# Paced table gathers, output tables on VectorE and scores in row halves, in a two-layer decoder trunk in float32

## The chip, the cores and the metric

One Trainium2 chip, one core. The metric is the time of one execution on the device, in microseconds (us). A trace is one execution taken by the hardware profiler; its span runs from the first to the last instruction, and the execution's own time is a little longer.

## The reference

256 tokens of width 1024 go through two layers. Each layer is: half a SwiGLU FFN (width 2816), a token mixer, half a second FFN, and a gated input embedding. Every sub-layer has a norm ahead of it and one behind. The mixer of layer 0 is differential attention with 8 heads of two maps each; that of layer 1 is a diagonal state-space model (S5) with 64 groups of 16 channels and 64 complex states, followed by GELU and a gated projection (GLU).

```python
# layer 0 mixer, per head, two maps m of 64 dimensions
s = einsum('bhmqd,bhmkd->bhmqk', q, k) + bias[t5_bucket(dist)]
prob = softmax(where(dist >= 0, s, -1e30))
attn = prob[:, :, 0] - lam * prob[:, :, 1]
o = rmsnorm(attn @ v, subln_g) * (1 - lambda_init)
m = o @ w_o
# layer 1 mixer, per group, complex diagonal recurrence
x[t] = a_bar * x[t-1] + b_bar @ u[t]
y[t] = (c @ x[t]).real + d * u[t]
z = gelu(y) @ w_glu + b_glu
m = z[:1024] * sigmoid(z[1024:])
```

## The kernel before

**Tiles and halves.** The tokens lie in two halves of 128 (b = 0 and 1). Each half is a generator (`thread(b)`), and a loop at the end of the program advances the two in steps, half 0 four to seven steps ahead (`lag`). One step of an FFN uses one weight unit of 512 KB: two slices of 128 rows, and for each three matmuls into 512 columns (`mm3`, L312 to L314).

**Weights.** Every float32 weight is loaded into a `raw` tile (SP's DMA queue, L124) and split into `hi` (ScalarE, L136) and `lo` = raw - hi (VectorE, L138). The three products hi x hi, lo x hi and hi x lo make up one float32 product. The class `Weights` takes loads up to 9 units (`NB`) ahead of half 1 (`W.next` is the next unit to load, `W.last_raw` the last load, `W.tiles` the split pairs); 9 split pairs and 3 raw tiles are kept.

**Order.** The program is ordered per engine ahead of the run by a list scheduler that simulates it, with priorities (`tc.high_priority`; a negative offset is a lower one). On the chip each engine then goes through its list in that order, and SP and GpSimd issue their DMAs from such lists. `tc.issue_after(i)` adds a dependence on instruction `i`.

**Norms.** `pre_norm` transposes x (L349), splits it (L331 on ScalarE, L332 on VectorE) and forms the factor on GpSimd (`v_pre`, `r_pre`, L325 and L327). `post_norm` squares on ScalarE (L380), forms `v_pn` and `r_pn` on GpSimd (L323, L327), and adds to x on VectorE (L387). The next `pre_norm` of that half begins with this x.

**Attention.** `attn_prepare` makes the table of biases in DRAM (`tab_d`) and two tiles `qz`, in which the two maps of a head's q stand in the upper and lower 64 rows with zeros in the other half. `scores(b, h)` does one head: a bias load on SP, two matmuls over all 128 rows (L596, two records each) into bank `a0` or `a1` by the parity of h, one addition, one maximum, two exponentials on ScalarE, and the combination of the maps on VectorE. `attend` (L619 to L625) uses the same banks.

**State-space tables.** `ssm_tables` is a generator. From the second FFN of layer 0 on, it is advanced at low priority at every second step of half 1 (`every`; a number yielded replaces it). For each of 8 group pairs `gp` it makes `vr`, `vi` by six products of 128x512 (L907 to L912, on GpSimd), transposes them (L933) and multiplies them in column quarters (L940) on TensorE, and stores `v_d`; then it makes `or`, `oi` by six further products on GpSimd in the same two tiles, and stores `o_d` from SP (L956). After that, eight DMAs write `m_d` (L972) and eight gathers of 512 KB build `t_d` from it (L975), all from GpSimd. `load_v` brings the first four `V` tiles in from SP (L1250), emitted when the loads come within 8 units of the mixer's first unit. The mixer of layer 1 reads `V`, `t_d` and `o_d`.

Of the kernel before, what the change touches and what calls it, by code (L numbers as in the profile page):

```python
# [9 lines left out]
F32 = mybir.dt.float32  # L10
# [3 lines left out]
ALU = mybir.AluOpType  # L14
# [54 lines left out]
TABLE_EVERY = OPT.get("every", 3)  # L69
PREPARE_AT = 36  # L70
# [77 lines left out]
def trunk(ctx, tc, x, p, norm_g, ffn_w_in, ffn_w_out, attn_w_qkv, attn_w_o, attn_lam, attn_subln_g,  # L148
# [377 lines left out]
    def attn_prepare():  # L526
        raw2_cm.__exit__(None, None, None)
        at_["pool"] = attn_pool_cm.__enter__()
        at_["qz"] = qz = [at_["pool"].tile([P, 4, 2, P], F32, tag=f"qz{b}", name=f"qz{b}", bufs=1) for b in range(2)]
        for b in range(2):  # L530
            nc.gpsimd.memset(qz[b][0:64, :, 1, :], 0.0)
            nc.gpsimd.memset(qz[b][64:128, :, 0, :], 0.0)
# [51 lines left out]
    def scores(b, h):  # L584
        kT = shared["kT"]
        nk = P * (b + 1)
        nm = f"{h}_{b}"
        bias = at_["pool"].tile([P, 2, 256], F32, tag="bias", name=f"bias{nm}", bufs=3)
        src = at_["tab_d"][2 * h:2 * h + 2, 256 - nk:256 - nk + 1]
        with tc.issue_after(W.last_raw.ins) if b == 0 and h < 3 else nullcontext():  # L590
            nc.sync.dma_start(bias[:, :, 0:nk], bass.AP(tensor=src.tensor, offset=src.offset,
                                                          ap=[[1, P], [384, 2], [1, nk]]))
        sp = bank(f"a{h % 2}", f"sp{nm}")
        spv = sp[:, :2 * nk].rearrange("p (m k) -> p m k", m=2)
        for m in range(2):
            nc.tensor.matmul(spv[:, m], at_["qz"][b][:, h % 4, m, :], kT[:, h, 0:nk], start=True, stop=True)  # L596
        s = at_["pool"].tile([P, 2, 256], F32, tag="s", name=f"s{nm}", bufs=3)
        sv = s[:, :, 0:nk]
        nc.vector.tensor_tensor(sv, spv, bias[:, :, 0:nk], ALU.add)
        mx = small.tile([P, 2], F32, tag="mx", name=f"mx{nm}")  # L600
        nc.vector.tensor_reduce(mx, sv, AX.X, ALU.max, negate=True)
        z = small.tile([P, 2], F32, tag="z", name=f"z{nm}")
        for m in range(2):
            nc.scalar.activation(s[:, m, 0:nk], s[:, m, 0:nk], AF.Exp, bias=mx[:, m:m + 1], accum_out=z[:, m:m + 1])
        rz = small.tile([P, 2], F32, tag="rz", name=f"rz{nm}")
        nc.vector.reciprocal(rz, z)
        c1 = small.tile([P, 1], F32, tag="c1", name=f"c1{nm}")
        nc.vector.tensor_tensor(c1, rz[:, 1:2], at_["neg_lam"], ALU.mult)
        at = weights_of(b, h)
        nc.vector.tensor_scalar(at, s[:, 0, 0:nk], rz[:, 0:1], None, ALU.mult)  # L610
        nc.vector.scalar_tensor_tensor(at, s[:, 1, 0:nk], c1, at, ALU.mult, ALU.add)
# [15 lines left out]
    def attention(b, qkv_units, pj_units, o_units):  # L627
# [33 lines left out]
        for n, (part, grp) in enumerate(QKV_ORDER):  # L661
# [21 lines left out]
            if part == 0:  # L683
                for m in range(2):
                    (nc.vector.tensor_copy if m >= OPT["qz"] else nc.scalar.copy)(
                        at_["qz"][b][64 * m:64 * m + 64, :, m, :], ptv[64 * m:64 * m + 64, :, ::-1])
            else:
                nc.vector.tensor_copy(kT[:, grp * 4:grp * 4 + 4, b * P:(b + 1) * P], ptv)
                for h in range(grp * 4, grp * 4 + 4):
                    with tc.high_priority(offset=HEAD_OFFSET):  # L690
                        scores(b, h)
# [74 lines left out]
    def ssm_tables(pool, keep):  # L766
# [137 lines left out]
        def products(out_r, out_i, ar_, ai_, br_, bi_, nm):  # L904
            g = nc.gpsimd
            t = pool.tile([P, 512], F32, tag="pt", name=f"pt{nm}", bufs=1).rearrange("p (q k h) -> p q k h", q=4, k=8)
# [11 lines left out]
        for gp in range(8):  # L918
# [4 lines left out]
            products(vr, vi, *A, *B, f"v{gp}")  # L923
# [24 lines left out]
            yield  # L948
# [395 lines left out]
```

## Time and profile before

| | |
|---|---|
| time, median of 3 runs (lowest to highest) | 1120.79 us (1118.37 to 1122.93) |
| profiled execution: time, span | 1120.96 us, 1119.2 us |
| busy: TensorE (PE), weight load (PEld) | 1043.0 us, 835.7 us |
| busy: VectorE (DVE), ScalarE (ACT), GpSimd (POOL) | 696.5 us, 553.8 us, 255.4 us |
| mean granted clock of TensorE | 0.975 of full |
| moved by DMA | 218.62 MB |

Busy times are sums over instructions of one engine. Matmuls overlap each other in the record, so the spacing of their starts tells more than their durations. Half 0 starts the gated embedding of layer 0 (`gt`, tiles `gtple`) at about 547 us, and the products of half 0 of the next FFN begin at about 590 us.

### The profile page before, as it was taken

What the parts mean: (1) busy time and instruction counts of PE and PEld (TensorE: products, weight loads), DVE (VectorE), ACT (ScalarE), POOL (GpSimd) and SP (SyncE); (2) the same over time, 40 slices, a digit from 0 to 9 for tenths busy, and PEclk for the clock granted to TensorE, in tenths of its full rate; (3) what the DMA queues carried; (4) which work ended last, traced back from release to release, by engine and by line L of the source; (5) the groups of instructions that cost most, each with busy time, mean ns of one, the idle gap of its engine ahead of it and who ended that gap; (6) DMA issues with size and microseconds to landing.
All of it is one profiled execution on the core that took longest, in us unless ns stands there. A gap on an engine that the chain in (4) does not pass through costs nothing. (4 is left out here: it accounts for less than half of the span.)

```text
span 1119.2 us, 14344 instructions
## 1 busy us (share of the span) xinstructions
PE 1043.0 (93%) x5123; PEld 835.7 (75%) x5123; DVE 696.5 (62%) x1011; ACT 553.8 (49%) x875; POOL 255.4 (23%) x315
## 2 busy tenths in 40 slices
PE   7999999999989999999778998999768899999996
PEld 5888888787766887777556886888546778888885
DVE  6656645688568986554686663654377676555464
ACT  6545444566655544443464543543335465444454
POOL 1002100100011018887788530000131010000001
PEclk9999999999999999999898999999989999999999
DMA  9656656476366777666564778766874647665651
GB/s 328 197 149 189 210 189 201 144 235 201 106 144 185 207 179 233 208 194 216 157 181 118 211 236 307 247 198 206 225 308 166 204 148 215 188 186 180 198 168 57
DMA packets 119816, 218.62 MB, mean 195 GB/s; under 512 B 25025, under 2 KB 43489, under 8 KB 119745
## 3 DMA queue, kind: packets, MB, share of 16 engines
q1 hardware_dynamic: 116864, 211.71, 60.9%
q0 software_dynamic: 1824, 5.33, 1.7%
q8 instruction: 40, 0.66, 0.2%
q10 hardware_dynamic: 1056, 0.66, 0.2%
q14 instruction: 32, 0.25, 0.1%
HBM read 205.13 MB, written 16.74 MB: 198 GB/s over the span
## 5 line engine op out<-in xcount | busy, mean ns | idle before, releaser
L138 DVE TENSOR_TENSOR lo<-raw,hi 128x1024 fp32r<-128x1024 f32 x332 | 429.6, 1301 | 266.3 <-ACT hi L136 264.7
L136 ACT CAST hi<-raw 128x1024 fp32r<-128x1024 f32 x332 | 347.3, 1052 | 327.1 <-PE up L314 106.5
L312 PE MATMUL up<-hi,xThi 128*128 128x512 f32 x704 | 279.3, 400 | 5.2 <-ACT hi L136 2.9
L313 PE MATMUL up<-lo,xThi 128*128 128x512 f32 x704 | 278.8, 397 | 1.5 <-DVE lo L138 1.4
L314 PE MATMUL up<-hi,xTlo 128*128 128x512 f32 x704 | 279.0, 400 | 0.0
L312 PEld LDWEIGHTS up<-hi,xThi 128*128 128x128 f32 x704 | 133.9, 190 | 34.8 <-ACT xThi L331 4.3
L313 PEld LDWEIGHTS up<-lo,xThi 128*128 128x128 f32 x704 | 134.1, 190 | 31.1 <-DVE lo L138 3.6
L314 PEld LDWEIGHTS up<-hi,xTlo 128*128 128x128 f32 x704 | 133.5, 191 | 28.1 <-issue 0.4
L312 PE MATMUL dn<-hi,hThi 128*128 128x512 f32 x352 | 139.2, 396 | 0.0
L313 PE MATMUL dn<-lo,hThi 128*128 128x512 f32 x352 | 138.5, 393 | 0.0
L314 PE MATMUL dn<-hi,hTlo 128*128 128x512 f32 x352 | 138.4, 394 | 0.0
L312 PEld LDWEIGHTS dn<-hi,hThi 128*128 128x128 f32 x352 | 66.8, 190 | 14.2 <-issue 0.6
L314 PEld LDWEIGHTS dn<-hi,hTlo 128*128 128x128 f32 x352 | 66.7, 190 | 14.3 <-issue 0.2
L313 PEld LDWEIGHTS dn<-lo,hThi 128*128 128x128 f32 x352 | 66.8, 190 | 13.6
L331 ACT ACTIVATE xThi<-xT_ps,gT 128x128 fp32r<-128x128 f32 x112 | 38.2, 368 | 59.2 <-PE xT_ps L349 58.3
L323 POOL TENSOR_SCALAR v_pn<-sspn,sspn 128x1 f32<-128x1 f32 x8 | 3.4, 422 | 246.8 <-ACT junkpn L380 244.7
L335 ACT CAST hThi<-hT_ps 128x512 fp32r<-128x512 f32 (+1 forms) x48 | 26.4, 550 | 56.2 <-PE hT_ps L459 56.0
L336 DVE TENSOR_TENSOR hTlo<-hT_ps,hThi 128x512 fp32r<-128x512 f32 (+1 forms) x48 | 30.8, 643 | 36.8 <-ACT hThi L335 36.7
L332 DVE SCALAR_TENSOR_TENSOR xTlo<-xT_ps,gT,xThi 128x128 fp32r<-128x128 f32 x112 | 36.1, 344 | 26.0 <-ACT xThi L331 25.5
L349 PE MATMUL xT_ps<-ident,x 128*128 128x128 f32 x112 | 30.3, 305 | 22.4 <-DVE xTlo L332 9.9
L349 PEld LDWEIGHTS xT_ps<-ident,x 128*128 128x128 f32 x112 | 16.2, 150 | 32.6 <-DVE xTlo L332 13.4
L456 DVE SCALAR_TENSOR_TENSOR h<-up,r_pre,sg 128x512 f32<-128x512 f32 (+1 forms) x48 | 33.6, 702 | 10.7 <-ACT sg L454 7.3
(360 smaller groups left out, 1319.5 us busy)
## 6 DMA issues: line engine op xcount, KB each, us to landing
raw<-in_ffn_w_in_dram SPq DMA_DIRECT2D x160, 512.0 KB, 4.4
raw<-in_ffn_w_out_dram SPq DMA_DIRECT2D x88, 512.0 KB, 3.9
raw<-in_attn_w_qkv_dram SPq DMA_DIRECT2D x24, 512.0 KB, 4.4
raw<-in_ffn_w_in_dram SPq DMA_DIRECT2D x32, 256.0 KB, 3.7
raw<-in_ple_w_gate_dram SPq DMA_DIRECT2D x16, 512.0 KB, 3.5
raw<-in_ssm_w_glu_dram SPq DMA_DIRECT2D x16, 512.0 KB, 4.1
gain<-in_norm_g_dram SPq DMA_DIRECT2D x8, 512.0 KB, 4.8
raw<-in_attn_w_o_dram SPq DMA_DIRECT2D x8, 512.0 KB, 4.2
```

The costliest lines, as they stand in the source:

```text
L136: nc.scalar.copy(hi, raw)
L138: (nc.gpsimd if n in self.on_pool else nc.vector).tensor_tensor(lo, raw, hi.bitcast(F32), ALU.subtract)
L312: nc.tensor.matmul(out_ap, st_hi, w_hi, start=start, stop=False)
L313: nc.tensor.matmul(out_ap, st_hi, w_lo, start=False, stop=False)
L314: nc.tensor.matmul(out_ap, st_lo, w_hi, start=False, stop=stop)
L323: nc.gpsimd.tensor_scalar(v, parts[0], parts[1], eps, ALU.add, ALU.add)
L331: return (nc.scalar.activation(hi, psum, AF.Copy, scale=scale).ins, nc.vector.scalar_tensor_tensor(lo, psum, scale, hi.bitcast(F32), ALU.m ...
L332: nc.vector.scalar_tensor_tensor(lo, psum, scale, hi.bitcast(F32), ALU.mult, ALU.subtract).ins)
L335: nc.scalar.copy(hi, psum)
L336: nc.vector.tensor_tensor(lo, psum, hi.bitcast(F32), ALU.subtract)
L349: marks[b].append(nc.tensor.transpose(pt, xb[:, k * P:(k + 1) * P], ident).ins)
L456: nc.vector.scalar_tensor_tensor(h[:, :w], up_, r, sg[:, :w], ALU.mult, ALU.mult)
```

## The change

It does four things.

Attention: `scores` takes two heads at a time. The `qz` tiles and their zeros go; q stands unpadded in one tile, written by one copy. Each map is a matmul over its own 64 rows, map 0 into bank `a0` and map 1 into bank `a1`, both heads side by side in a bank. The bias load, the maximum, the reciprocal and the factor are done once for two heads.

Tables: the six products for `or`, `oi` go from GpSimd to VectorE, with tiles of their own (`or`, `oi`, `po`). The generator is advanced every third step of half 1 during the group pairs.

Gathers: the `m_d` writes wait until the loads have come 24 units into the first FFN of layer 1. Each `t_d` gather is bound to a one-element copy on GpSimd that reads the newest split tile, and one is emitted every four steps.

V loads: from 16 units ahead of the mixer's first unit on, one load per step, each bound to the last weight load. The scratch for GpSimd's DMA descriptors is set to 8192 bytes.

```diff
+V_AHEAD = 16
+TD_FROM = 24
@@ attn_prepare
-        at_["qz"] = qz = [at_["pool"].tile([P, 4, 2, P], F32, tag=f"qz{b}", name=f"qz{b}", bufs=1) for b in range(2)]
-        for b in range(2):
-            nc.gpsimd.memset(qz[b][0:64, :, 1, :], 0.0)
-            nc.gpsimd.memset(qz[b][64:128, :, 0, :], 0.0)
+        at_["q"] = [at_["pool"].tile([P, 4, P], F32, tag=f"q{b}", name=f"q{b}", bufs=1) for b in range(2)]
@@ scores
-    def scores(b, h):
+    def scores(b, h0):
+        kT, q = shared["kT"], at_["q"][b]
...
+        bias = at_["pool"].tile([P, 2, 2, 256], F32, tag="bias", name=f"bias{nm}", bufs=2)
+        src = at_["tab_d"][2 * h0:2 * h0 + 4, 256 - nk:256 - nk + 1]
+        with tc.issue_after(W.last_raw.ins) if b == 0 and h0 < 4 else nullcontext():
+            nc.sync.dma_start(bias.rearrange("p h m k -> p (h m) k")[:, :, 0:nk], bass.AP(
+                tensor=src.tensor, offset=src.offset, ap=[[1, P], [384, 4], [1, nk]]))
-        sp = bank(f"a{h % 2}", f"sp{nm}")
-        spv = sp[:, :2 * nk].rearrange("p (m k) -> p m k", m=2)
-        for m in range(2):
-            nc.tensor.matmul(spv[:, m], at_["qz"][b][:, h % 4, m, :], kT[:, h, 0:nk], start=True, stop=True)
+        sp = [bank(f"a{m}", f"sp{nm}{m}")[:, :2 * nk].rearrange("p (h k) -> p h k", h=2) for m in range(2)]
+        for h in range(2):
+            for m in range(2):
+                rows = slice(64 * m, 64 * m + 64)
+                nc.tensor.matmul(sp[m][:, h], q[rows, (h0 + h) % 4, :], kT[rows, h0 + h, 0:nk], start=True, stop=True,
+                                 skip_group_check=True)
+        s = at_["pool"].tile([P, 2, 2, 256], F32, tag="s", name=f"s{nm}", bufs=2)
         for m in range(2):
+            nc.vector.tensor_tensor(s[:, :, m, 0:nk], sp[m], bias[:, :, m, 0:nk], ALU.add)
+        mx = small.tile([P, 4], F32, tag="mx", name=f"mx{nm}")
+        nc.vector.tensor_reduce(mx, s.rearrange("p h m k -> p (h m) k")[:, :, 0:nk], AX.X, ALU.max, negate=True)
...
@@ attention
-                for m in range(2):
-                    (nc.vector.tensor_copy if m >= OPT["qz"] else nc.scalar.copy)(
-                        at_["qz"][b][64 * m:64 * m + 64, :, m, :], ptv[64 * m:64 * m + 64, :, ::-1])
+                nc.vector.tensor_copy(at_["q"][b], ptv[:, :, ::-1])
...
-                for h in range(grp * 4, grp * 4 + 4):
+                for h in range(grp * 4, grp * 4 + 4, 2):
                     with tc.high_priority(offset=HEAD_OFFSET):
                         scores(b, h)
@@ ssm_tables
-        def products(out_r, out_i, ar_, ai_, br_, bi_, nm):
-            g = nc.gpsimd
-            t = pool.tile([P, 512], F32, tag="pt", name=f"pt{nm}", bufs=1).rearrange("p (q k h) -> p q k h", q=4, k=8)
+        def products(g, tag, out_r, out_i, ar_, ai_, br_, bi_, nm):
+            t = pool.tile([P, 512], F32, tag=tag, name=f"pt{nm}", bufs=1).rearrange("p (q k h) -> p q k h", q=4, k=8)
...
-            products(vr, vi, *A, *B, f"v{gp}")
+            products(nc.gpsimd, "pt", vr, vi, *A, *B, f"v{gp}")
...
-            yield
-            o_r = pool.tile(shp, F32, tag="vr", name=f"or{gp}", bufs=1)
-            o_i = pool.tile(shp, F32, tag="vi", name=f"oi{gp}", bufs=1)
+            yield 3
+            o_r = pool.tile(shp, F32, tag="or", name=f"or{gp}", bufs=1)
+            o_i = pool.tile(shp, F32, tag="oi", name=f"oi{gp}", bufs=1)
...
-            products(o_r, o_i, *A, *C, f"o{gp}")
+            products(v, "po", o_r, o_i, *A, *C, f"o{gp}")
...
-            yield
+            yield 3
...
-        yield 1
+        while W.next < flat(plan[("ffn", 1, 0)])[0] + TD_FROM:
+            yield 1
         for k in range(8):
             nc.gpsimd.dma_start(m_d[:, :, 7 + k, :], m16[16 * k:16 * k + 16])
         yield 2
+        pace = pool.tile([1, 8], F32, tag="zt", name="pace", bufs=1)
         for s_ in range(8):
-            nc.gpsimd.dma_start(t_d[16 * s_:16 * s_ + 16].rearrange("i g (c x) -> i (g c) x", x=P),
+            n = max(W.tiles)
+            gate = nc.gpsimd.tensor_copy(pace[:, s_:s_ + 1], W.tiles[n][0].bitcast(F32)[0:1, 0:1])
+            with tc.issue_after(gate.ins):
+              nc.gpsimd.dma_start(t_d[16 * s_:16 * s_ + 16].rearrange("i g (c x) -> i (g c) x", x=P),
                               m_d.rearrange("i g k o -> i g (k o)")[:, :, 16 * s_:16 * s_ + P])
-            yield 2
+            yield 4
@@ load_v and the loop over the steps
-                nc.sync.dma_start(ssm["V", pr][j], v_d[2 * pr + j])
+                with tc.issue_after(W.last_raw.ins):
+                    nc.sync.dma_start(ssm["V", pr][j], v_d[2 * pr + j])
+                yield
...
-        if has_ssm and "pool" in ssm and ("V", 0) not in ssm and W.next >= plan[("ssm",)][0][0] - OPT["vl"]:
-            load_v()
+        if has_ssm and "pool" in ssm and b == 1 and W.next >= plan[("ssm",)][0][0] - V_AHEAD:
+            ssm.setdefault("loads", load_v())
+            next(ssm["loads"], None)
...
-    nc = _bacc.Bacc("TRN2", target_bir_lowering=False, num_devices=1)
+    nc = _bacc.Bacc("TRN2", target_bir_lowering=False, num_devices=1, dynamic_dma_scratch_size=8192)
```

## Rows read from the trace of the kernel before

**Rows 1.** Page, busy us (share) and instructions; then span and granted clock.

```profile
PE 1043.0 (93%) x5123; PEld 835.7 (75%) x5123; DVE 696.5 (62%) x1011; ACT 553.8 (49%) x875; POOL 255.4 (23%) x315
...
core 0: 1119.2 us, clock 0.975
```

**Rows 2.** Windows of three stretches; columns as in the first line.

```profile
core 0: us, PE busy (x) PEld busy (x) DVE busy (x) ACT busy (x) POOL busy (x), PEclk, DMA share, GB/s
413.00:545.00 132.00, 121.76 (x612) 95.50 (x611) 74.55 (x58) 56.80 (x78) 108.76 (x85) 0.98 0.68 206
520.00:620.00 100.00, 81.82 (x383) 60.18 (x382) 65.37 (x71) 50.47 (x95) 78.93 (x70) 0.88 0.51 149
680.00:700.00 20.00, 16.94 (x67) 13.21 (x68) 9.48 (x10) 8.90 (x10) 0.00 (x0) 0.91 0.80 272
```

**Rows 3.** TensorE groups, 520 to 620 us, last 440 to 520: busy, mean, idle.

```profile
L349 PE MATMUL xT_ps<-ident,x 128*128 128x128 f32 x30 | 9.0, 316 | 12.4 <-DVE xTlo L332 8.6 <-DVE x L387 3.8
...
L933 PE MATMUL v_ps<-ident,vi 128*128 128x128 f32 x16 | 4.4, 298 | 5.5 <-POOL vi L912 5.5
...
L933 PE MATMUL v_ps<-ident,vi 128*128 128x128 f32 x12 | 3.1, 286 | 4.1 <-POOL vi L912 4.1
```

**Rows 4.** Timeline of GpSimd: start us, us, operation.

```profile
413.74 1.28 POOL L910 TENSOR_TENSOR vi<-ai,br 128x512 f32<-128x512 f32 x1
...
539.40 1.27 POOL L323 TENSOR_SCALAR v_pn<-sspn,sspn 128x1 f32<-128x1 f32 x1
540.65 1.25 POOL L912 TENSOR_TENSOR oi<-oi,pto 128x512 f32<-128x512 f32 x1
541.87 0.57 POOL L327 TENSOR_TENSOR r_pn<-v_pn,neg_half 128x1 f32<-128x1 f32 x1
...
624.94 1.66 POOL L912 TENSOR_TENSOR oi<-oi,pto 128x512 f32<-128x512 f32 x1
```

**Rows 5.** By line, ns min/median/max: 440 to 640 us, L1128 whole span.

```profile
L910 POOL TENSOR_TENSOR oi<-ai,cre x7: 1099/1111/2090, 460.1 to 619.0; 128x512 f32<-128x512 f32 x7
...
L138 DVE TENSOR_TENSOR lo<-raw,hi x51: 1207/1655/2353, 439.6 to 635.7; 128x1024 fp32r<-128x1024 f32 x51
...
L1128 DVE TENSOR_TENSOR rthi<-rtlo,er x2: 679/679/679, 823.3 to 839.8; 128x512 f32<-128x512 f32 x2
...
L1128 DVE TENSOR_TENSOR rt<-rt,er x2: 1034/1040/1046, 830.3 to 846.1; 128x512 f32<-128x512 f32 x2
...
L383 DVE TENSOR_TENSOR ygpnple<-mple,gain x4: 1522/1586/1779, 571.5 to 599.2; 128x512 f32<-128x512 f32 x4
```

**Rows 6.** Timeline of GpSimd: the gathers, and its next work for others.

```profile
665.44 6.01 POOL L975 DMA_DIRECT2D t_d<-m_d  x8 [3.46 <-DMA m_d<-msb]
...
787.79 0.35 POOL L990 MEMSET ssm_sel<- 128x128 f32 x2 [115.83 <-PE dn L314]
```

**Rows 7.** Groups, TensorE, 680 to 700 us.

```profile
L312 PE MATMUL up<-hi,xThi 128*128 128x512 f32 x22 | 9.1, 434 | 2.9 <-ACT hi L136 2.9
...
L313 PE MATMUL up<-lo,xThi 128*128 128x512 f32 x20 | 8.6, 428 | 0.8 <-DVE lo L138 0.8
```

**Rows 8.** Timeline of TensorE around the products of two heads, half 1.

```profile
244.08 0.39 PE L313 MATMUL qkvat<-lo,xThi 128*128 128x512 f32 x1
244.31 1.89 PE L596 MATMUL sp<-attn_hi,qz 128*128 128x256 f32 x8
...
246.49 0.39 PE L313 MATMUL qkvat<-lo,xThi 128*128 128x512 f32 x1
```

**Rows 9.** Timeline of TensorE around four products in column quarters.

```profile
518.82 0.39 PE L314 MATMUL dn<-hi,hTlo 128*128 128x512 f32 x1
...
520.18 0.40 PE L314 MATMUL dn<-hi,hTlo 128*128 128x512 f32 x1
...
520.62 0.43 PE L940 MATMUL m_ps<-vr,cp 128*32 128x128 f32 x8
...
521.56 0.40 PE L314 MATMUL dn<-hi,hTlo 128*128 128x512 f32 x1
```

More of the change, by code (lines that the diff above doesn't have):

```diff
@@ L582, in weights_of @@
         return shared["at"][h] if b else shared["at"][8 + h // 2][:, (h % 2) * P:(h % 2) * P + P]
-    def scores(b, h):
-        kT = shared["kT"]
+    def scores(b, h0):
+        kT, q = shared["kT"], at_["q"][b]
         nk = P * (b + 1)
[L587 to L592, printed above, removed]
-        sp = bank(f"a{h % 2}", f"sp{nm}")
-        spv = sp[:, :2 * nk].rearrange("p (m k) -> p m k", m=2)
-        for m in range(2):
-            nc.tensor.matmul(spv[:, m], at_["qz"][b][:, h % 4, m, :], kT[:, h, 0:nk], start=True, stop=True)
[L597 to L602, printed above, removed]
-        for m in range(2):
-            nc.scalar.activation(s[:, m, 0:nk], s[:, m, 0:nk], AF.Exp, bias=mx[:, m:m + 1], accum_out=z[:, m:m + 1])
-        rz = small.tile([P, 2], F32, tag="rz", name=f"rz{nm}")
-        nc.vector.reciprocal(rz, z)
[L607 to L611, printed above, removed]
@@ new lines, in scores @@
+        nm = f"{h0}_{b}"
+        bias = at_["pool"].tile([P, 2, 2, 256], F32, tag="bias", name=f"bias{nm}", bufs=2)
[4 more added lines that the diff above has]
+        sp = [bank(f"a{m}", f"sp{nm}{m}")[:, :2 * nk].rearrange("p (h k) -> p h k", h=2) for m in range(2)]
@@ new lines, in scores @@
+        nc.vector.tensor_reduce(mx, s.rearrange("p h m k -> p (h m) k")[:, :, 0:nk], AX.X, ALU.max, negate=True)
+        z = small.tile([P, 4], F32, tag="z", name=f"z{nm}")
+        for j in range(4):
+            part = s[:, j // 2, j % 2, 0:nk]
+            nc.scalar.activation(part, part, AF.Exp, bias=mx[:, j:j + 1], accum_out=z[:, j:j + 1])
+        rz = small.tile([P, 4], F32, tag="rz", name=f"rz{nm}")
+        nc.vector.reciprocal(rz, z)
+        c1 = small.tile([P, 2], F32, tag="c1", name=f"c1{nm}")
@@ L613, in attend @@
+        nc.vector.tensor_scalar(c1, rz.rearrange("p (h m) -> p h m", m=2)[:, :, 1], at_["neg_lam"], None, ALU.mult)
+        for h in range(2):
+            at = weights_of(b, h0 + h)
+            nc.vector.tensor_scalar(at, s[:, h, 0, 0:nk], rz[:, 2 * h:2 * h + 1], None, ALU.mult)
+            nc.vector.scalar_tensor_tensor(at, s[:, h, 1, 0:nk], c1[:, h:h + 1], at, ALU.mult, ALU.add)
     def attend(b, h, on):
@@ L1306, in trunk @@
             tables_step()
-        if has_ssm and "pool" in ssm and ("V", 0) not in ssm and W.next >= plan[("ssm",)][0][0] - OPT["vl"]:
-            load_v()
+        if has_ssm and "pool" in ssm and b == 1 and W.next >= plan[("ssm",)][0][0] - V_AHEAD:
+            ssm.setdefault("loads", load_v())
+            next(ssm["loads"], None)
         if state == ["join", "join"]:
             end_tables()
-            if ("V", 0) not in ssm:
-                load_v()
+            for _ in ssm.setdefault("loads", load_v()):
+                pass
             pool = ssm["pool"]
```

## The prediction

> **What bounds the kernel now.** I read the busy times first, then the windows along the span, then for each window in which TensorE is not full the groups that were idle before they ran, and last the order of time on the engine that was waited for. TensorE works 1043.0 of 1119.2 us at a mean granted clock of 0.975 [rows 1], so a change can win in two ways only: by closing its 76 us of gaps, or by keeping its clock at the upper of the two levels (2.4 GHz). The reader should see where those gaps lie. From 520 to 620 us it works 81.8 of 100 us at a clock of 0.88, and from 680 to 700 us 16.9 of 20 at 0.91 [rows 2]. In the first of these the idle time is 12.4 us ahead of the transposes of x at L349 and 5.5 us ahead of the transposes of `vi` at L933, and there are another 4.1 us of the latter kind from 440 to 520 [rows 3].
>
> What is late there is GpSimd. It makes the state-space tables: per group six products for `v` and six for `o`, 96 in all, from 413.7 to 626.6 us [rows 4]. TensorE meets each `v` inside the stream of weights, in an order fixed ahead of the run, and stands until the product lands. The norms suffer too: `v_pn` and `r_pn`, which release x, stand between two products (539.4, then a product at 540.7, then 541.9) [rows 4]. Each product is slower than it need be: one form takes between 1.10 and 2.09 us, and VectorE's split `lo` between 1.21 and 2.35 us in the same stretch [rows 5]. Both are drawn out by about one instruction of the other engine, so the two engines take turns.
>
> In the second place the eight gathers of `t_d` leave GpSimd within 6.0 us [rows 6], weights come late, and TensorE waits 2.9 and 0.8 us for a split [rows 7].
>
> **The change, part by part.**
>
> *Output tables on VectorE.* 48 of the 96 products leave GpSimd, and `or`/`oi` get tiles of their own, so `v` of the next group need not wait until `o` has gone out. A group now comes every six steps of half 1 in place of four. A step is one weight unit for both token halves: 2 slices x 3 products x 2 halves = 12 products. From 518.82 to 520.18 us seven of them start 0.227 us apart [rows 9], so a step is 2.72 us, six are 16.3 us, and eight groups 131 us. Begun at 414 us they end near 545 us, about where the chain behind the waits of L349 begins; before, they ran to 627 us, through the whole of that chain.
>
> Waits for `v`: 4.1 + 5.5 = 9.6 us. Between two meetings GpSimd ran twelve products and now runs six, so half the overrun (4.8 us) would stay; the longer period takes some more. I keep 3 and win 6.6.
>
> Waits of the norms: 12.4 us, in four places. I keep 1 us for each and win 8.4.
>
> Clock: 100 us at 0.88 mean 12.0 us not granted [rows 2]. It fell behind the longer of those waits. I keep 3 and win 9.
>
> Together 24.0; bounds: half of the 34.0 us there, 17, if the tables still reach into the norms, and all 34.0.
>
> *What VectorE pays.* The trace has no such product on VectorE. The nearest rows are products of 128x512 out of SBUF: 0.68 us free, 1.04 beside some GpSimd work, 1.59 in the thick of it [rows 5]. 48 of them cost 33, 50 or 76 us. From 413 to 545 us VectorE is busy 74.6 of 132 us [rows 2], so 57.4 are free. I take 1.04, since GpSimd will run half its products: 50 us fit, at 94%. I charge 2.5 us for splits that come late behind such a product, between 0 and the 19 us by which 76 overshoots. Behind a late product on SP stand the `o_d` stores, and behind these weight loads; raw and split buffers cover that, and without them it is the same late split.
>
> *Paced gathers.* Each gather waits on GpSimd for a one-element copy of the newest split. They start when the loads are 24 units into the next FFN (half 1 nine units behind, unit 15), then one every four steps, 10.9 us, for 76 us in place of 6. Behind the waiting copy on GpSimd stand only further gathers and set-up: its next work for anyone else was at 787.8 us [rows 6]. The four V loads, held behind a weight load each, follow at about half 1's step 46 of the 66 of that FFN. Removed: 2.9 + 0.8 us and 20 x 0.09 = 1.8 us of clock [rows 2, 7], 5.5 in all; a lone gather of 0.5 MB beside a weight load may still cost something, so I win 5.0 (between 4 and 5.5). If V came late instead, the first state products wait; 20 steps, 54 us, stand between. The halved DMA scratch is taken at nothing: if descriptors wait for room, only GpSimd's idle stretch pays.
>
> *Scores in row halves.* Before, the products of two heads of half 1 stand among weight products that would have taken 3 x 0.227 = 0.68 us alone and take 246.49 - 244.08 = 2.41 [rows 8]: 1.73 us, 0.86 a head. Half 0 has half as many columns, so 0.43. Eight heads of each make 10.3 us. If the two row halves run side by side this halves, a gain of 5.2; if in turn, nothing. The trace shows no row halves, only column quarters: one transpose and four such products stretch three products' 0.68 us to 1.38, by 0.70 [rows 9]. Four products of 128 columns one after another would cost 0.86 (two heads of half 0), so the quarters do overlap; a perfect overlap is 0.22, and at most 0.48 goes for getting in and out. Eight pairs x 0.48 = 3.8. Net 1.4, between 5.2 and -3.8.
>
> The Trainium skill, TensorEngine Tiling (Array Packing), section Key Properties, says against this part that a change of tiling mode drains the array. The trace agrees as far as the 0.48 us goes. By a full drain at each pair and no overlap this term would be -3.8 in place of 1.4.
>
> A pair now fills both banks `a0` and `a1`, so the next pair waits for both additions where heads alternated. QKV products of the other half hide that; uncovered it is two additions of about 0.68 [rows 5] per pair, 11 us in all, which I take at nothing. The single copy for q, the shared reductions and reciprocals, the absent memsets and the half as many bias loads on SP only relieve VectorE, GpSimd and SP; no gap listed above ends on them, so they too count nothing.
>
> **Sum.** The profiled execution took 1120.96 us, its span 1119.2 and 1.8 around it, 0.2 from the median of 1120.79. 1120.96 - 24.0 - 5.0 - 1.4 + 2.5 = 1093.1, say 1093.
>
> **Rivals.**
>
> *The shared door stays full.* Taking turns, not GpSimd's count, may be what sets the pace. From 413.7 to 626.6 us a group took 26.6 us. At free prices it cost 12 x 1.10 for products and, at the 51 splits in 200 us of [rows 5], 6.8 splits at 1.21: 21.4 of 26.6 us. Afterwards 6 x 1.10 + 6 x 0.68 and 4.2 splits (at that rate) to 6 (one a step) at 1.21 make 15.8 to 17.9 of 16.3 us: fuller than before. For it speaks how much both engines are drawn out [rows 5]; against it, that VectorE falls behind without TensorE standing as long as split buffers last. Then half of the 24.0 is won: 1120.96 - 12 - 5 - 1.4 + 2.5 = 1105.
>
> The Trainium skill, SBUF — State Buffer, section SBUF: two separate sides, states this as a rule: the port pair that VectorE and GpSimd share is an exclusive lock, held for the whole instruction, when the VectorE instruction has two SBUF inputs. The trace agrees (2.09 against 1.10 us), and by it the time would be that 1105.
>
> *The tables are not what is late.* The norms of this stage have few matmuls beside them, and their chains over ScalarE and VectorE could be long without GpSimd. Then only the gathers and the scores pay: 1120.96 - 5 - 1.4 + 2.5 = 1117. Against it, GpSimd stands directly in the chain at 539 to 542 us [rows 4].
>
> *VectorE becomes the bound: slower.* It decides where 48 products exceed the 57.4 us free, at 1.20 us each. At the 1.59 us row they overrun by 19 us; splits come late by that much, the loop again runs into the norms so that nothing of the 24.0 is won, and the clock falls as it does now, 12.0 us for 17.9 us of waits, another 12.7. 1120.96 + 19 + 12.7 - 5 - 1.4 = 1146. Against it, with GpSimd half empty the thick case should be the rarer.
>
> **Chances.** Forecast 0.63, full door 0.17, only the gathers 0.11, VectorE the bound 0.09. A difference of 0.5%, 5.6 us, is about what a measurement of this kernel can tell from none. The first two are faster (0.80), the third within 0.5% (0.11), the fourth slower (0.09). The forecast's own range is 1076 (34.0 + 5.5 + 5.2 won, nothing paid) to 1108 (17 + 4 won, 3.8 + 4 paid). The range reaches to the third case, 1076 to 1117, and leaves out the slow one and a little at either end.
>
> **What would show it.** Right: GpSimd's busy time down by 70 us or more from 255; the last table product near 545 us, not 627; `lo` in that stretch nearer 1.4 than 1.66 us; waits of L933 below 4 us and of L349 in the next norms below 5; clock above 0.95 there and 0.98 overall; the gathers spread over 70 us and no wait for a split at 680; a pair of half 1 costing about 1.2 us of TensorE. Wrong: table products on VectorE of 1.5 us, waits of TensorE for `lo` or `hTlo` from 413 to 545 us, tables that still run at 600 us, score pairs costing as much as before or waits at the additions. A new order of instructions elsewhere that opens gaps of its own would make the total wrong with every step right.

## The result and the profile after

The kernel after takes 1104.28 us (median of 4 runs, 1103.19 to 1107.41), the kernel before 1119.58 on the same chip: a ratio of 0.986, interval 0.984 to 0.988. It is faster (the interval is clear of 1) and inside the range, but by 15.3 us where 28 were forecast. The profiled execution took 1104.01 us. Line numbers are higher by one to six than before's (L349 is now L351, L933 is L934).

The page of after, as [rows 1]:

```profile
PE 1039.9 (94%) x5123; PEld 831.6 (75%) x5123; DVE 704.5 (64%) x1031; ACT 554.9 (50%) x875; POOL 196.1 (18%) x271
...
core 0: 1102.2 us, clock 0.976
```

Busy times don't say where 17.0 us of span went. I numbered the weight products of TensorE (128x512) in the order of its timeline; they are the same work in every version, 3984 of them in every trace. Counted off a timeline whose rows merge several products, a landmark is good to some 0.7 us. The time between two landmarks, us, for every profiled execution of this study (one per kernel):

| kernel | 900 to 1300, attention | 1300 to 2200, tables and norms | 2400 to 2500, gathers | 2500 to 3100, state part | ratio to before, interval |
|---|---|---|---|---|---|
| before | 134.4 | 266.8 | 29.8 | 194.5 | 1 |
| after | 138.4 | 253.1 | 23.6 | 193.7 | 0.986 (0.984 to 0.988) |
| e1_old_scores | 134.5 | 254.4 | 23.6 | 192.2 | 0.981 (0.978 to 0.984) |
| e2_o_bound | 140.9 | 255.6 | 23.7 | 191.0 | 0.983 (0.979 to 0.988) |
| e5_both | 135.2 | 250.1 | 23.6 | 196.1 | 0.980 (0.978 to 0.983) |
| e4_no_gate | 142.3 | 249.6 | 23.6 | 191.7 | 0.983 (0.980 to 0.987) |
| e6_pairs_padded | 137.3 | 252.1 | 23.6 | 194.7 | 0.984 (0.982 to 0.986) |
| e7_single_halves | 145.2 | 254.3 | 23.6 | 191.6 | 0.989 (0.986 to 0.991) |
| e8_paced_only | 134.7 | 265.1 | 23.7 | 195.0 | 0.996 (0.994 to 0.998) |
| e9_v_only | 135.5 | 265.6 | 24.5 | 196.0 | 0.996 (0.995 to 0.998) |
| e10_o_gpsimd | 140.8 | 276.6 | 23.6 | 191.2 | 1.006 (1.004 to 1.008) |
| e11_late_d | 135.1 | 252.2 | 23.6 | 197.6 | 0.983 (0.981 to 0.985) |
| e12_five_steps | 134.7 | 251.9 | 23.7 | 197.3 | 0.983 (0.981 to 0.985) |
| e13_no_o | 134.6 | 248.9 | 23.6 | 190.3 | 0.976 (0.974 to 0.978) |

So after wins 13.7 us with the tables (forecast 21.5, the 24.0 less VectorE's 2.5) and 6.2 with the gathers (5.0), and loses 4.0 in attention (a gain of 1.4). Windows of after, as [rows 2]:

```profile
core 0: us, PE busy (x) PEld busy (x) DVE busy (x) ACT busy (x) POOL busy (x), PEclk, DMA share, GB/s
413.00:545.00 132.00, 126.49 (x643) 98.37 (x641) 102.11 (x112) 58.66 (x79) 78.22 (x61) 0.99 0.73 224
520.00:620.00 100.00, 91.63 (x453) 68.34 (x452) 62.67 (x92) 58.01 (x106) 59.76 (x66) 0.95 0.58 172
680.00:700.00 20.00, 20.00 (x93) 16.55 (x92) 10.71 (x12) 9.13 (x10) 2.75 (x4) 1.00 0.74 243
```

From 520 to 620 us TensorE works 9.8 us more and is granted 7 us more of its clock, and at 680 us it is full. Its groups from 520 to 620 us, as [rows 3]:

```profile
L351 PE MATMUL xT_ps<-ident,x 128*128 128x128 f32 x32 | 9.4, 302 | 4.1 <-DVE xTlo L334 2.7 <-DVE x L389 1.3
...
L934 PE MATMUL v_ps<-ident,vi 128*128 128x128 f32 x16 | 4.3, 294 | 1.1 <-POOL vi L913 1.1
...
L941 PE MATMUL m_ps<-vr,cp 128*32 128x128 f32 x32 | 1.7, 285 | 1.2 <-POOL vr L910 1.2
```

The waits of L351 fell from 12.4 to 4.1 us, those for `vr` and `vi` from 5.5 to 2.3, and none of the latter stands from 440 to 520 us. But GpSimd did not do its work where the prediction put it. Its timeline, as [rows 4] and [rows 6]:

```profile
441.97 0.18 POOL L916 MEMSET zt<- 16x112 f32 x1 [43.65 <-DVE cmb L723]
...
443.41 5.36 POOL L911 TENSOR_TENSOR vi<-ai,br 128x512 f32<-128x512 f32 x1
...
568.76 1.60 POOL L913 TENSOR_TENSOR vi<-vi,ptv 128x512 f32<-128x512 f32 x1
...
645.92 0.78 POOL L981 DMA_DIRECT2D t_d<-m_d  x1
...
726.56 0.76 POOL L981 DMA_DIRECT2D t_d<-m_d  x1
```

The products for `v` run from 443 to 570 us, not from 414 to 545, because the end of the `b` tables on VectorE (`cmb`, then `bi`, the last at 445.0 us; in before at 413.6) comes late. What VectorE did instead, groups from 395 to 495 us:

```profile
L140 DVE TENSOR_TENSOR lo<-raw,hi 128x1024 fp32r<-128x1024 f32 x31 | 41.8, 1348 | 4.7 <-ACT hi L138 4.7
L913 DVE TENSOR_TENSOR oi<-oi,pto 128x512 f32<-128x512 f32 x8 | 7.5, 942 | 0.0
...
L908 DVE TENSOR_TENSOR or<-ar,cre 128x512 f32<-128x512 f32 x7 | 6.8, 967 | 0.1
```

All the `o` products but two, which ran at 361 and 366 us, stand in these 100 us (the six groups of rows sum to 39.3 us for 46, 0.85 each), and VectorE is busy 95.1 of them. They need the powers and `c`, not `b`, so the compiled order puts them ahead of the `b` tables. What TensorE then waits for:

```profile
469.17 0.44 PE L461 MATMUL hT_ps<-ident,h 128*128 128x128 f32 x2 [2.02 <-DVE h L458]
474.69 0.33 PE L461 MATMUL hT_ps<-ident,h 128*128 128x128 f32 x1 [0.87 <-DVE h L458]
...
488.67 0.50 PE L315 MATMUL dn<-lo,hThi 128*128 128x512 f32 x1 [1.32 <-DVE lo L140]
```

These 4.2 us, with a granted clock of 0.91 from 460 to 480 us (1.8 us), are what VectorE pays: 6.0 where 2.5 were charged.

### The profile page after: what moved, and what is told of

Read it like the earlier page. It is cut to its first block, busy times and chain, and to the rows that moved or that the text cites. A ratio compares the mean times of both kernels' runs of the same rounds, so it can differ in the third digit from the quotient of the medians.

```text
span 1102.2 us, 14301 instructions
## 1 busy us (share of the span) xinstructions
PE 1039.9 (94%) x5123; PEld 831.6 (75%) x5123; DVE 704.5 (64%) x1031; ACT 554.9 (50%) x875; POOL 196.1 (18%) x271
## 4 chain that ended last, share of the span: by engine, by line
PE 58%; issue 20%; DVE 10%; DMA 6%; ACT 3%; POOL 2%; SPq 1%; DVEq 0%; POOLq 0%; ACTq 0%
PE up L316 9%; PE up L315 9%; PE up L314 9%; PE dn L315 5%; PE dn L314 5%; PE dn L316 5%; DMA raw<-in_ffn_w_in_dram 3%; DVE lo L140 3%; PE qkvat L314 2%; PE qkvat L315 2%; PE qkvat L316 2%; ACT hi L138 1%; PE hT_ps L461 1%; PE xT_ps L351 1%; PE zglu L314 1%
## 5 line engine op out<-in xcount | busy, mean ns | idle before, releaser
L140 DVE TENSOR_TENSOR lo<-raw,hi 128x1024 fp32r<-128x1024 f32 x332 | 413.4, 1251 | 242.9 <-ACT hi L138 239.8
L314 PE MATMUL up<-hi,xThi 128*128 128x512 f32 x704 | 276.4, 397 | 3.3 <-ACT xThi L333 3.2
L333 ACT ACTIVATE xThi<-xT_ps,gT 128x128 fp32r<-128x128 f32 x112 | 38.3, 368 | 39.3 <-PE xT_ps L351 37.9
L351 PE MATMUL xT_ps<-ident,x 128*128 128x128 f32 x112 | 30.0, 298 | 13.5 <-DVE xTlo L334 6.0
L458 DVE SCALAR_TENSOR_TENSOR h<-up,r_pre,sg 128x512 f32<-128x512 f32 (+1 forms) x48 | 33.7, 702 | 10.9 <-ACT sg L456 6.8
L314 PE MATMUL qkvat<-hi,xThi 128*128 128x512 f32 x96 | 39.1, 407 | 0.3 <-ACT xThi L333 0.3
```

The costliest lines, as they stand in the source:

```text
L140: (nc.gpsimd if n in self.on_pool else nc.vector).tensor_tensor(lo, raw, hi.bitcast(F32), ALU.subtract)
L314: nc.tensor.matmul(out_ap, st_hi, w_hi, start=start, stop=False)
L333: return (nc.scalar.activation(hi, psum, AF.Copy, scale=scale).ins, nc.vector.scalar_tensor_tensor(lo, psum, scale, hi.bitcast(F32), ALU.m ...
L351: marks[b].append(nc.tensor.transpose(pt, xb[:, k * P:(k + 1) * P], ident).ins)
L458: nc.vector.scalar_tensor_tensor(h[:, :w], up_, r, sg[:, :w], ALU.mult, ALU.mult)
```

## The experiments

**Attention.** Three kernels take the pairs apart. The first goes back to before's scores:

```diff
-        sp = [bank(f"a{m}", ...) for m in range(2)]
-                nc.tensor.matmul(sp[m][:, h], q[rows, (h0 + h) % 4, :], kT[rows, h0 + h, 0:nk], ...)
+        sp = bank(f"a{h % 2}", f"sp{nm}")
+            nc.tensor.matmul(spv[:, m], at_["qz"][b][:, h % 4, m, :], kT[:, h, 0:nk], ...)
```

> The kernel after with the attention scores of the kernel before (zero-padded rows, one head at a time). Theory: the pairs cost TensorE 4 us between 227 and 365 us of the trace (landmarks of the weight products), so this version takes 1104 - 4 = about 1100 us, and its landmark at the end of that stretch stands 3 to 5 us earlier than after's. Rival: the 4 us come from how the rest of the list was reordered (loads, VectorE), and the scores themselves are neutral or win the 1.4 us of the forecast: 1104 to 1106 us.

Measured: 1102.37 us beside 1123.70 of before, 0.981 to after's 0.986. The attention stretch is back at 134.5 us. The theory holds: the new scores cost this stretch 4 us, where 1.4 were to be won.

The second keeps the pairs and drops the row halves, the third keeps the row halves and drops the pairs:

```diff
 e6_pairs_padded, against after
+        sp = [bank(f"a{h}", ...)[:, :2 * nk] ... for h in range(2)]
+                nc.tensor.matmul(sp[h][:, m], qz[:, (h0 + h) % 4, m, :], kT[:, h0 + h, 0:nk], ...)
 e7_single_halves, against e1
+        sp = [bank(f"a{m}", f"sp{nm}{m}")[:, :nk] for m in range(2)]
+            nc.tensor.matmul(sp[m], at_["q"][b][rows, h % 4, :], kT[rows, h, 0:nk], ...)
```

> The kernel after with its pairs of heads (shared reductions, two banks, one bias load per pair) but with zero-padded products of 128 rows, one bank per head. The measure is the time between the 900th and the 1300th weight product: 134.4 us in before, 138.4 in after. Theory A, pairing is what costs (a pair holds both banks until both additions are done, and its softmax is twice as long before the first head can go on): 138 to 142 us here. Theory B, the products in row halves cost (getting in and out of them): 134 to 136 us here.

> The kernel after with one head at a time, each head two products of 64 rows in the two halves of the array, into two banks. Same measure. Theory A, pairing costs: 134 to 137 us here, since a single head's chain is as short as before (it still holds both banks, which could bring it to 137). Theory B, row halves cost, and twice as often as in pairs: 139 to 145 us.

Measured: 137.3 and 145.2 us, to before's 134.4. Neither theory alone survives: pairing costs 1.8 to 2.9 us without any row half (against the 134.4 to 135.5 of all executions with single padded heads), row halves cost too, and entered head by head they cost most (8.6 of those 10.8 us are clock, 0.91, 0.75 and 0.91 granted in three windows of 20 us). TensorE around two products of half 0, after first (with VectorE's addition between the two groups of one pair), then e6_pairs_padded:

```profile
254.32 0.71 PE L597 MATMUL sp<-attn_hi,q 64*128 64x128 f32 x4
...
255.92 0.42 DVE L601 TENSOR_TENSOR s<-sp,bias 128x256 f32<-128x256 f32 x1
...
256.69 0.39 PE L314 MATMUL qkvat<-hi,xThi 128*128 128x512 f32 x1
257.00 0.71 PE L597 MATMUL sp<-attn_hi,q 64*128 64x128 f32 x4
...
257.98 0.39 PE L316 MATMUL qkvat<-hi,xTlo 128*128 128x512 f32 x1
```

```profile
255.43 0.39 PE L315 MATMUL qkvat<-lo,xThi 128*128 128x512 f32 x1
255.66 0.60 PE L599 MATMUL sp<-attn_hi,qz 128*128 128x128 f32 x4
...
256.33 0.40 PE L314 MATMUL qkvat<-hi,xThi 128*128 128x512 f32 x1
```

From the weight product ahead to the second one behind is 1.29 us in row halves and 0.90 padded; less two weight products (0.455) the scores took 0.84 and 0.45 us. In half 0 the row halves thus cost nearly twice as much. The group of after is not a head: the addition at 255.92 us takes one map of both heads (128x256) and runs before the second group of its pair starts, so a group is one map of two heads. Three of the four pairs of half 0 are split like this by other products. Their row halves do not run side by side, and each of the six groups pays for getting in and out. In half 1 a pair stays together and wins. The same stretch of after, two heads, to be held against [rows 8]:

```profile
242.84 0.39 PE L314 MATMUL qkvat<-hi,xThi 128*128 128x512 f32 x1
243.16 1.13 PE L597 MATMUL sp<-attn_hi,q 64*128 64x256 f32 x8
...
244.56 0.40 PE L316 MATMUL qkvat<-hi,xTlo 128*128 128x512 f32 x1
```

That is 1.72 less 0.455, 1.27 us, where the padded two took 1.73. At these prices the six groups of half 0 lose 2.3 us and the two pairs of half 1 in the stream of weights win 0.9: a loss of 1.4. After stands 1.1 above e6_pairs_padded, but executions of one attention code differ by more (138.4 to 142.3, below), so the landmarks alone do not show it. In e7_single_halves both maps of a head (four records) take no longer than one map alone (two):

```profile
254.97 0.39 PE L316 MATMUL qkvat<-hi,xTlo 128*128 128x512 f32 x1
255.28 0.70 PE L595 MATMUL sp<-attn_hi,q 64*128 64x256 f32 x4
...
256.25 0.39 PE L315 MATMUL qkvat<-lo,xThi 128*128 128x512 f32 x1
...
260.37 0.39 PE L315 MATMUL qkvat<-lo,xThi 128*128 128x512 f32 x1
260.69 0.70 PE L595 MATMUL sp<-attn_hi,q 64*128 64x256 f32 x2
...
261.65 0.39 PE L314 MATMUL qkvat<-hi,xThi 128*128 128x512 f32 x1
```

Both take 1.28 us, 0.83 net, so the two row halves do run side by side. A second head adds 1.27 - 0.83 = 0.44 us, which leaves 0.83 - 0.44 = 0.39 us for getting in and out: an estimate from these rows, below the prediction's 0.48. The Trainium skill, TensorEngine Tiling (Array Packing), section Key Properties, says that changing the mode drains the array; these 0.39 us agree.

The rest of what the pairs cost is waits and clock, in shares that differ by execution. TensorE of after waits longer for a softmax of two heads:

```profile
284.16 0.33 PE L623 MATMUL aT_ps<-ident,at 128*128 128x128 f32 x1 [1.97 <-DVE s L601]
```

All its waits from 227 to 366 us sum to 11.5 us, in before to 8.6, in e6_pairs_padded to 10.1. But in the three other executions of after's attention code they sum to 8.8 to 9.4, and in the eight with single padded heads to 7.6 to 9.4. What those three lose instead is clock: 6.8 to 8.5 us in this stretch, against 1.7 in after and 0 to 1.7 in the eight. Windows of after, then of e4_no_gate, whose attention is the same code:

```profile
280.00:285.00 5.00, 2.51 (x12) 1.59 (x11) 3.46 (x8) 3.33 (x12) 0.00 (x0) 1.00 0.00 0
285.00:290.00 5.00, 5.00 (x16) 3.96 (x15) 3.94 (x11) 3.22 (x10) 0.00 (x0) 0.66 0.00 0
```

```profile
275.00:280.00 5.00, 3.66 (x14) 2.42 (x14) 1.99 (x3) 2.98 (x12) 1.25 (x2) 0.74 0.57 201
280.00:285.00 5.00, 5.00 (x14) 3.44 (x14) 3.12 (x5) 2.58 (x10) 0.00 (x0) 0.50 0.00 1
285.00:290.00 5.00, 4.62 (x13) 3.10 (x11) 4.25 (x9) 2.12 (x9) 0.00 (x0) 0.50 0.00 0
```

After loses 1.7 us of clock here, e4_no_gate 6.3 (the lower level, 1.2 GHz, for 12.6 of these fifteen). In e4_no_gate the clock fell before the softmax was waited for, behind another wait:

```profile
276.13 0.33 PE L623 MATMUL aT_ps<-ident,at 128*128 128x128 f32 x1 [1.55 <-ACT onat L629]
```

After has the same 1.55 us at 275.24 and kept its clock there, so which wait the clock falls behind differs by execution; why it then stays down longer with the new scores is not shown. In the eight executions with single padded heads the stretch takes 134.4 to 135.5 us, in the four with pairs in row halves 138.4 to 142.3: the new scores cost some 3 to 8 us, and more the longer the clock stays down. (In after 2.9 us of waits, 1.7 of clock and 1.4 of row halves make 6.0, not 4.0; what offsets the rest I did not trace.)

**The order on VectorE.** The `o` products are held behind their group's `msb`, alone and with the old scores:

```diff
+            oo = pool.tile([P, 3, 4, 8, 16], F32, tag="or", ...)
+            o_r, o_i = oo[:, 0], oo[:, 1]
+            v.tensor_copy(oo[0:1, :, 0, 0, 0], msb[0:1, gp, 0, 0, 0:3])
-            products(v, "po", o_r, o_i, *A, *C, f"o{gp}")
+            products(v, "po", o_r, o_i, *A, *C, f"o{gp}", oo[:, 2])
```

> The kernel after with each group's output products held behind that group's msb by a copy of three elements, so that they follow the b tables on VectorE instead of preceding them. Theory: the 46 output products that ran from 397 to 490 us held VectorE at 20 of 20 us and delayed bi and with it GpSimd's v products by 30 us. Held back, the v products start near 415 us and end near 545 us, the 4.2 us of TensorE waits between 469 and 489 us go, and so do most of those between 543 and 597 us: 1092 to 1098 us. Rival, the shared door stays full: VectorE and GpSimd draw each other out instead, v products become slower than 1.2 us each, the loop still ends at 560 us or later and the time stays at 1101 to 1106 us.

> The kernel after with both edits: old scores and the output products held behind msb. Theory: the two gains add, 1104 - 4 - (6 to 12) = 1088 to 1094 us, faster than both kernels. Rival: without the 4 us of attention the tables start later against the stream of weights, and half of the first gain is lost again: 1092 to 1098 us. If neither edit matters it stays at 1104 us.

Measured: 1106.36 and 1101.03 us beside 1123.70, 0.983 and 0.980; by these ratios some 1101 and 1097 us where before takes 1119.58, the rivals' times and not the theories'. The order did what was expected: in e5_both TensorE has no waits from 363 to 520 us and the last `vi` begins at 537.3; in e2_o_bound at 547.9. The gain did not follow. In e2_o_bound the stretch of the tables takes 255.6 us: one product for `vi` was drawn out to 5.20 us and TensorE stood 2.67 us for it. In e5_both it takes 250.1, 4.3 less than in e1_old_scores, which has the same scores, and 3 less than in after. The norms wait nearly as in before; TensorE of e5_both, 557 to 583 us:

```profile
558.04 0.33 PE L351 MATMUL xT_ps<-ident,x 128*128 128x128 f32 x1 [0.82 <-DVE xTlo L334]
560.70 0.73 PE L316 MATMUL gtple<-hi,xTlo 128*128 128x512 f32 x2 [0.95 <-DVE xTlo L334]
...
578.95 0.59 PE L351 MATMUL xT_ps<-ident,x 128*128 128x128 f32 x2 [2.85 <-DVE xTlo L334]
```

GpSimd's last `vi` was long done by then. All waits from 520 to 640 us sum to 11.8 us here, to 8.2 in after and 18.0 in before. So the theory of the 6 to 12 us fell. e5_both gains mostly what the old scores give: with 0.980 its interval is clear of after's, but not of e1_old_scores' 0.981.

Two further versions went at those waits, first by moving the small instructions for `ssm_d` out of the norms, then by a period of five steps on top:

```diff
+        while W.next < flat(plan[("ffn", 1, 0)])[0] + 10:
+            yield 1
         m16 = msb.rearrange("p g e q h -> p (g e q) h")
 e12 also, ahead of the o products
-            yield 3
+            yield 2
```

> Old scores and output products held behind msb, and in addition the part with ssm_d (four times two loads and three small VectorE instructions) held until the loads are ten units into the next FFN. Theory: those instructions stand on VectorE between 560 and 589 us among the xTlo splits that TensorE waits for, so the 10.6 us of waits left between 538 and 592 us fall to 6 to 8: 0.975 to 0.979 of before. Rival: those waits are the norms' own chain over ScalarE, GpSimd and VectorE: no change, 0.979 to 0.982.

> As the version with the late ssm_d part, and a period of five steps a group in place of six. Theory: the last two groups of tables still stand in the norms; at 13.6 us a group the loop ends near 520 us, the stretch between product 1900 and 2200 falls from 94.8 us to 88 to 91, total 0.972 to 0.977 of before. Rival, the shared door: GpSimd's six products at 1.75 us beside VectorE and 3.2 us of cp copies make 13.7 us of a 13.6 us period, so vi is late again, TensorE waits for it 5 to 10 us between 413 and 520 us, total 0.980 to 0.986.

Measured: both 0.983. Waits from 520 to 640 us are 14.6 and 11.9 us, so the `ssm_d` instructions were not what was late. A comparison of all runs says more. The idle time ahead of the transposes of x from 520 to 660 us, in e5_both, then in e10_o_gpsimd (below), where all 96 products are on GpSimd again:

```profile
L351 PE MATMUL xT_ps<-ident,x 128*128 128x128 f32 x32 | 9.3, 300 | 9.4 <-DVE xTlo L334 8.0 <-DVE x L389 1.4
...
L351 PE MATMUL xT_ps<-ident,x 128*128 128x128 f32 x32 | 9.1, 296 | 3.1 <-DVE xTlo L334 3.1
```

With before's attention code it is 10.9 to 12.4 us in the three versions with all products on GpSimd and 7.3 to 10.9 in the five without the `o` products there; in the six with any other attention code it is 3.1 to 4.4 (of these, e2_o_bound waits as long again for `xThi` and `xTlo` elsewhere). So this wait goes mainly with the attention code, probably by the order that the scheduler then makes, which no run tests, and only by some 3 us with GpSimd's work. The period of five steps tested nothing: the last `vi` began at 536.1 us, with six steps at 537.6.

**What the move itself is worth.** The `o` products go back to GpSimd, all else as in after; and, on the base of e11_late_d, they are left out:

```diff
 e10_o_gpsimd
-            products(v, "po", o_r, o_i, *A, *C, f"o{gp}")
+            products(nc.gpsimd, "po", o_r, o_i, *A, *C, f"o{gp}")
 e13_no_o
-            products(v, "po", o_r, o_i, *A, *C, f"o{gp}", oo[:, 2])
+            v.memset(oo[:, 0:2], 0.0)
```

> The kernel after with the output products back on GpSimd; their own tiles, the period of six steps, the paced gathers and the pairs stay. The measure is the time between the 1900th and the 2200th weight product (norms and first per-layer block), 111.3 us in before and 95.8 in after. Theory: what wins there is that 48 products leave GpSimd. With 96 on it at 1.4 to 1.7 us each a group needs 22 to 26 us, the loop runs past 600 us, and the stretch takes 107 to 113 us: total 0.995 to 1.003 of before. Rival: the own tiles and the new period are enough: 95 to 99 us, total 0.984 to 0.989 of before.

> As the version with the late ssm_d part, but the 48 output products are left out (their tiles are filled with zeros, so the state-space output lacks that part); stores, order and everything else stay. It prices the products on VectorE. Theory: VectorE pays little once they are spread: the stretch between product 1300 and 1900 is unchanged (155 us, no waits there) and 1900 to 2200 falls by 2 to 4 us: total 2 to 4 us below the version that has them. Rival: they still draw GpSimd and the splits out: v products fall from 1.7 to 1.3 us or less, the loop ends 10 us earlier, and the total is 6 to 10 us lower.

Measured: e10_o_gpsimd 1127.26 us beside 1121.23, 1.006. The move to VectorE is worth 2.0%, 22 us, but not where the theory had it: the stretch from product 1900 to 2200 took 94.3 us, as the rival said (95.8 in after), and the loss came before. Three groups of `o` and the start of a fourth ran on GpSimd ahead of the first `vi`. TensorE waited for VectorE's splits beside them, and then for `vr` and `vi`, which came late:

```profile
425.23 0.50 PE L315 MATMUL up<-lo,xThi 128*128 128x512 f32 x1 [2.02 <-DVE lo L140]
...
431.23 0.50 PE L315 MATMUL up<-lo,xThi 128*128 128x512 f32 x1 [2.95 <-DVE lo L140]
...
451.19 0.33 PE L934 MATMUL v_ps<-ident,vr 128*128 128x128 f32 x1 [3.97 <-POOL vr L910]
...
508.60 0.47 PE L934 MATMUL v_ps<-ident,vr 128*128 128x128 f32 x1 [5.25 <-POOL vr L910]
```

Its waits from 363 to 520 us sum to 20.8 us, in after to 4.2. Of the 20.8, 13.0 are for `vr` and `vi` and 6.4 for splits, so the theory's cause (too many products on GpSimd) held, in another stretch than it named.

e13_no_o: 1093.93 us, 0.976, 7.6 us below e11_late_d; the two profiled executions differ by 10.9. In the stretch of the tables 3.3 of these fall, which is what spread products cost on VectorE beyond the zeros written in their place, near the theory's 2 to 4. GpSimd's own products took 1.55 us on average, in e11_late_d 1.71: drawn out less, not set free. Another 7.3 lie in the state part, so that the total is the rival's, 6 to 10, but not by its mechanism: e11_late_d has there a wait of 3.65 us for `x` near 879 us, and its clock loses 5 us more from 690 to 900 us. Six of the fourteen executions have the like of that wait (3.65 to 4.04 us, before among them), after has 0.94 us and e13_no_o none. It stands long after the tables; why it comes and goes stays open.

**Gathers and V loads.** The first kernel is after with the gathers sent as before; the other two are before with one edit each:

```diff
 e4_no_gate, against after
-        while W.next < flat(plan[("ffn", 1, 0)])[0] + TD_FROM:
-            gate = nc.gpsimd.tensor_copy(pace[:, s_:s_ + 1], ...)
 e8_paced_only, against before
+        while W.next < flat(plan[("ffn", 1, 0)])[0] + TD_FROM:
+            gate = nc.gpsimd.tensor_copy(pace[:, s_:s_ + 1], ...)
 e9_v_only, against before
+                with tc.issue_after(W.last_raw.ins):
+                    nc.sync.dma_start(ssm["V", pr][j], v_d[2 * pr + j])
+                yield
```

> The kernel after with the gathers of t_d sent as before (no waiting for unit 24 of the next FFN, no copy ahead of each, one every two steps). Theory: pacing alone is worth the 6.2 us that the landmarks show between 660 and 720 us, so this takes 1109 to 1111 us and TensorE waits for a split behind the gathers again. Rival: the gathers got room because the tables end earlier and not because they are paced: 1104 us, with the gathers spread anyway.

> The kernel before with nothing but the paced gathers of t_d (unit 24, a copy ahead of each, four steps apart). The measure is the time between the 2400th and the 2500th weight product, 29.8 us in before and 23.6 in after. Theory: the loss was the collision of eight gathers with the four V loads in one stretch of 6 us, and either move ends it: 23.6 to 24.5 us, total 5 to 6 us below before. Rival, the gathers alone were harmless and the four V loads in a lump did it: V now leaves in a lump after the last gather, and the loss only moves to a later stretch: total within 2 us of before.

> The kernel before with nothing but the V loads sent one per step, each behind a weight load; the gathers leave in a burst as before. Same measure. Theory of the collision: 23.6 to 25 us, total 4 to 6 us below before. Rival, the burst of gathers is enough by itself to make the weights late: 28 to 30 us, total within 2 us of before.

Measured: the stretch from product 2400 to 2500 takes 23.6, 23.7 and 24.5 us, to before's 29.8; the ratios of the two edits to before are both 0.996, 4 to 5 us. For e4_no_gate the theory fell. Its gathers left in a burst, earlier, and its V loads apart from them:

```profile
620.77 5.28 POOL L976 DMA_DIRECT2D t_d<-m_d  x7 [3.81 <-DMA m_d<-msb]
626.76 0.76 POOL L976 DMA_DIRECT2D t_d<-m_d  x1 [0.71 <-issue]
```

TensorE waited 0.29 us behind it. In before the four V loads (2 MB) left SP's queue at 665.28 us, 0.16 us ahead of the eight gathers (4 MB), and the 2.9 and 0.8 us of [rows 7] followed. Windows of e8_paced_only and e9_v_only:

```profile
680.00:700.00 20.00, 20.00 (x93) 16.55 (x92) 11.37 (x11) 9.71 (x11) 3.45 (x4) 1.00 0.75 236
```

```profile
680.00:700.00 20.00, 19.50 (x90) 15.63 (x89) 11.94 (x12) 9.55 (x12) 0.00 (x0) 1.00 0.77 250
```

So it was the collision: either of the two moves ends it.

## Why the prediction was right in sign and off in size

**Relieving GpSimd: right nearly to size, in part by luck.** Of the waits for `v`, 2.3 us remain (3 kept), of the norms' 4.1 (4 kept), of the clock from 520 to 620 us 5.0 (3 kept): 22.6 won of the 24.0. The waits for `v` are GpSimd's: with all products back on it they rise to 13.0 us before 520 us alone. The norms' 8.3 us are so for some 3 at most, as the versions compare. With GpSimd relieved and its tables done by 539 us, e5_both and e13_no_o still wait 9.4 and 7.3 us there; with GpSimd full, e10_o_gpsimd waits 3.1. The rest of that fall goes with the new attention code, which the prediction gave no part in it ("no gap listed above ends on them").

**"Begun at 414 us they end near 545 us": this step failed.** It took the new order on VectorE to be the program's, spread over 132 us. VectorE got the `o` products as soon as their own inputs were there, all 48 before 487 us, and `b` and all of GpSimd's work came 30 us later, to end at 570 us. The price per product was below the one taken (0.85, not 1.04), the sum fitted the free time, and TensorE paid all the same, 6.0 us for 2.5, because the products came in one dense stretch. Some 1.8 us of new waits for `xThi` in the norms (0.78, 0.58 and 0.46) complete the difference: 22.6 - 6.0 - 1.8 is 14.8, to 13.7 by the landmarks. Yet repairing the order took away those waits for VectorE and gave little: 4.3 us of this stretch with the old scores, a loss of 2.5 with the pairs, and in the whole time nothing clear of noise (0.981 to 0.980, 0.986 to 0.983). What was left in the norms did not hang on the tables.

**"Which I take at nothing" (the next pair's wait for both banks), and "only relieve": the wrong step of the scores.** Pairs lengthen the chain from the scores to the transposes: 2.9 us more waits and 1.7 us of clock in after, no more waits but 6.8 to 8.5 us of clock in the three other executions of this code. Of row halves, the pair of half 1 was right (1.27 us, some 1.2 forecast), and so was the price of getting in and out (0.39, at most 0.48). What the sum left out is that a pair can be pulled apart: in three of the four pairs of half 0 the two maps stand apart, and a group takes 0.84 us where 0.45 stood.

**Gathers: right in size, wrong in cause.** 6.2 us for 5.0; but the V loads, counted at nothing, were the other half of the collision, and either edit alone brings this gain, to within 1 us. The smaller descriptor scratch, also taken at nothing, was not run by itself.

**Rivals.** "The shared door stays full" gave 1105 us, closest to the result, and its row was right: GpSimd's `v` products took 1.65 us on average in after, with half the work gone, and 1.62 before (1.48 to 1.72 in the other versions). But fullness did not set the time: GpSimd sat idle 19.6 us in front of its `vr` products, waiting for TensorE's transposes of the group before, and without any `o` product (e13_no_o) its products still took 1.55. The Trainium skill, SBUF — State Buffer, section SBUF: two separate sides, calls the shared ports an exclusive lock. The product of 5.36 us at 443.4 us fits that, for VectorE was busy 5.40 of 5.40 us beside it; but eight of its instructions ran in that time, so here the two did not take turns, as the prediction had it. "The tables are not what is late" is refuted for the waits for `v`; for most of the norms' waits the runs speak for it. "VectorE becomes the bound" named the right mechanism (VectorE late, 2.9 us for `h` and 1.3 for a split, and lost clock) and came in at 6.0 us, not at its 19 and 12.7. Of the signs, GpSimd's busy time fell by 59 us and not 70; the eight new copies ahead of the gathers take 9.9 us of the difference.

## What to carry to other kernels

When work moves to another engine, ask what its inputs are, not where it stands in the program: an instruction that is ready early runs early, and in front of what matters. A three-element copy that makes it depend on the right thing is enough to place it; whether that pays is another question (here hardly).

Before pairing small products for the array's sake, follow the chain behind them: the softmax of two heads comes as one, the products can be pulled apart by others, and the clock may fall behind a wait and stay down. When transfers come late, list everything that is issued in the same few microseconds before pacing one of them.

## What the runs showed of the hardware

- Products of 64 rows in the two row halves ran side by side: 0.83 us of TensorE for one map and for two (e7_single_halves). Some 0.39 us of it, an estimate, is for entering and leaving them between 128-row products.
- The same attention code took 138.4 to 142.3 us; from 275 to 290 us the granted clock cost 1.7 us in after and 6.3 in e4_no_gate.
- Half as many GpSimd products did not make each much faster (1.62 us before, 1.65 after, 1.55 with no `o` products on VectorE).
- 2 MB of V loads issued 0.16 us ahead of 4 MB of gathers cost TensorE some 6 us of late weights; either set alone cost less than 1 us (e4_no_gate, e8_paced_only, e9_v_only).
